# mLSTM scan on one Trainium2 core: states of both directions first, then each chunk once for both

## The chip, the core and the metric

The program runs on one core of one Trainium2 chip. The metric is device time in microseconds (us), from the launch to the end of the program; smaller is better. Five engines work side by side, each with its own queue in its own order: TensorE (PE; its weight loads are listed apart as PEld), VectorE (DVE), ScalarE (ACT), GpSimd (POOL) and SyncE (SP), which issues the transfers. Semaphores tie the queues together.

## The reference, cut to what matters

The program is a two-layer block model (an mLSTM layer and a retention layer, each with a mixture of experts), followed by a block of attention and feed-forward. The change touches the mLSTM scan alone: 8 heads, key width 64, value width 128, 256 context and 512 latent positions, forward and backward. The queries, keys and values of the two directions are the same; only the gates differ. The reference takes chunks of 64 positions.

```python
def mlstm_scan(q, k, v, ig, lf, state):
...
    def step(carry, inp):
        C, n, m = carry
        qc, kc, vc, ic, fc = inp
        b = jnp.cumsum(fc, axis=-1)
        dmat = jnp.where(tril, b[..., :, None] - b[..., None, :] + ic[..., None, :], -jnp.inf)
        inter = b + m[..., None]
        m_row = jnp.maximum(inter, dmat.max(-1))
        s = jnp.einsum('bhid,bhjd->bhij', qc, kc) * jnp.exp(dmat - m_row[..., None])
        w_inter = jnp.exp(inter - m_row)
        num = jnp.einsum('bhij,bhjv->bhiv', s, vc) + w_inter[..., None] * jnp.einsum('bhid,bhdv->bhiv', qc, C)
        den = s.sum(-1) + w_inter * jnp.einsum('bhid,bhd->bhi', qc, n)
        h = num / jnp.maximum(jnp.abs(den), jnp.exp(-m_row))[..., None]
...
        C_new = wc[..., None, None] * C + jnp.einsum('bhj,bhjd,bhjv->bhdv', wk, kc, vc)
...
    oc_f, s = scan_f(ctx_f, state0)
    ol_f, _ = scan_f(lat_f, s)
    oc_b, s = scan_b(flip(ctx_b), state0)
    ol_b, _ = scan_b(flip(lat_b), s)
    return oc_f + jnp.flip(oc_b, 2), ol_f + jnp.flip(ol_b, 2)
...
        y = y * lax.rsqrt(jnp.mean(y * y, axis=-1, keepdims=True) + EPS)
        y = y.reshape(b_, t_, h_ * d_) * norm_g.astype(f32) * jax.nn.sigmoid(o.astype(f32))
```

## The kernel before, in words

The kernel runs the scan in six chunks of 128 positions (two of context, four of latent). `mlstm` (L369) projects the inputs: `qk` holds queries (column blocks 0 to 3) and keys (4 to 7) transposed, two heads of 64 rows to a block of 128 partitions; `v` holds the values with a 129th column for the denominator; `sigo` holds the output gate. `mlstm_gates` (L486) makes from the gates, for both directions, the small tables that the scan reads: `rowt`, `wint` (as three bf16 parts), `colt`, `wk`, `em`, `wcc`, the causal mask, the selectors `sel3`, and `hm`, two columns that are one on the upper or the lower 64 partitions.

`mlstm_scan` (L599) goes through six steps `s`; in each it takes one chunk forward and one backward (orders 0 to 5, and 1, 0, 5, 4, 3, 2), each in two halves `g` of four heads: 24 units. A unit makes the exponents' rows (`rb`, L621 and L623, bf16), keys masked to one head's 64 rows (`kz`, L627, ACT), the products `sc` of keys and queries (L631, over all 128 partitions, the other head's rows being zero), W = Exp (L634, ACT, one per head), P = `sc` times W (L636, DVE); from step 1 on `qb` (L641) and the weighted, masked queries `qw` (L645, DVE); up to step 4 the new state: transposed keys `kt` (L650), `kw` (L652, DVE), `kv` (L657), and C (L662, DVE). Then per pair of heads `o` = P·v (L669) plus `qw`·C (L671), the denominator (Abs on ACT, L673; maximum and reciprocal on DVE), and `o` over the denominator into `y`, or into `yt` and added by POOL or DVE when the other direction came first (L678, L680). After a chunk's second visit `mlstm_finish` (L692) squares `y` (ACT), sums (DVE), takes Sqrt (`rstd`, L95; ACT loads another table for it, and Exp's again after it) and multiplies gate and norm in (POOL L700, L701, DVE L703).

`fill(2)` (L138) advances `ada_mix` (L204) between units: eight weight loads of 1 MB through a ring of four slots, their matmuls L216, and a last step. `ada_close` runs what is left of it after the scan. Buffers: `sc` 2, `rb` 1, `mm` 2 (shared by `qb`, `kt` and `kv`), `o` 2, one for `ada_mix`: eight PSUM banks. A planner at build time sets the order on each engine from the program's order, the buffers and estimated durations, so units are interleaved in the queues. What comes next is `moe0` (L904) with the output projection; its memory is what the scan's inputs leave free.

Of the kernel before, what the change touches and what calls it, by code (L numbers as in the profile page):

```python
# [6 lines left out]
F32 = mybir.dt.float32  # L7
# [5 lines left out]
ALU = mybir.AluOpType  # L13
# [34 lines left out]
class Net:  # L48
# [83 lines left out]

    def ada_close(self):
        self.fill(1000)
        self.aps.close()
        self.ap.close()
# [232 lines left out]
    def mlstm(self):  # L369
# [113 lines left out]
        self.ada_close()  # L483
        return yp, y

    def mlstm_gates(self, G, gp):  # L486
# [16 lines left out]
        hm = gp.tile([128, 2], F32, name="hm")  # L503
        nc.vector.memset(hm, 0.0)
        nc.vector.memset(hm[0:64, 0:1], 1.0)
        nc.vector.memset(hm[64:128, 1:2], 1.0)
# [90 lines left out]
        self.gates = sel3, hm, mask, dirs  # L597

    def mlstm_scan(self, qk, v, gates, y, sigo):  # L599


        nc, I = self.nc, self.I
        NC = 6
        sel3, hm, mask, dirs = gates
        wpool = self.pool("sc_w", 2)
        ng = wpool.tile([128, D], F32, name="ng", bufs=1)
        nc.sync.dma_start(ng, I["mlstm_head_norm_g"][0].partition_broadcast(128))
        pso = self.pool("sc_pso", 2, space=PSUM)
        ps = self.pool("sc_ps", 1, space=PSUM)
        tok = lambda c: slice(128 * c, 128 * c + 128) if c < 2 else slice(128 * c + 2, 128 * c + 130)  # L610
        state = {}
        seen = set()
        for s in range(NC):
            for d in range(2):
                order, rowt, wint, colt, wk, em, wcc = dirs[d]
                c = order[s]
                for g in range(2):
                    pairs = (2 * g, 2 * g + 1)
                    sc = ps.tile([128, 2, 2, 128], F32, name="sc", bufs=2)
                    rb = ps.tile([128, 4, 128], F32, name="rb")  # L620
                    nc.tensor.matmul(rb, self.identb, mask[:, d], start=True, stop=False)  # L621
                    for a in range(4):
                        nc.tensor.matmul(rb[:, a, :], sel3[:, 4 * g + a, :], rowt[:, 128 * c:128 * c + 128],  # L623
                                         start=False, stop=a == 3)
                    kz = wpool.tile([128, 2, 2, 128], F32, name="kz")
                    for e in range(2):
                        nc.scalar.activation(kz[:, :, e, :], qk[:, 4 + 2 * g:6 + 2 * g, tok(c)], AF.Copy,  # L627
                                             scale=hm[:, e:e + 1])
                    for a, p in enumerate(pairs):
                        for e in range(2):  # L630
                            nc.tensor.matmul(sc[:, a, e, :], kz[:, a, e, :], qk[:, p, tok(c)], start=True, stop=True)  # L631
                    W = wpool.tile([128, 4, 128], F32, name="W")
                    for a in range(4):
                        nc.scalar.activation(W[:, a, :], rb[:, a, :], AF.Exp, bias=colt[:, c, 4 * g + a:4 * g + a + 1])  # L634
                    P = wpool.tile([128, 2, 2, 128], F32, name="P")
                    nc.vector.tensor_tensor(P.rearrange("p a e i -> p (a e) i"), sc.rearrange("p a e i -> p (a e) i"), W,  # L636
                                            ALU.mult)
                    if s:
                        qb = ps.tile([128, 2, 128], F32, name="mm", bufs=2)
                        for a, p in enumerate(pairs):  # L640
                            nc.tensor.matmul(qb[:, a, :], sel3[:, 8 + p, :], wint[:, 128 * c:128 * c + 128],  # L641
                                             start=True, stop=True)
                        qw = wpool.tile([128, 2, 2, 128], F32, name="qw")
                        for e in range(2):
                            nc.vector.scalar_tensor_tensor(qw[:, :, e, :], qk[:, 2 * g:2 * g + 2, tok(c)], hm[:, e:e + 1],  # L645
                                                           qb, ALU.mult, ALU.mult)
                    if s < NC - 1:
                        kt = ps.tile([128, 2, 128], F32, name="mm", bufs=2)
                        for a, p in enumerate(pairs):
                            nc.tensor.transpose(kt[:, a, :], qk[:, 4 + p, tok(c)], self.ident)  # L650
                        kw = wpool.tile([128, 4, 64], F32, name="kw")
                        nc.vector.tensor_tensor(kw, kt.rearrange("p a (b e) -> p (a b) e", b=2),  # L652
                                                wk[:, c, 4 * g:4 * g + 4][:, :, None].to_broadcast([128, 4, 64]),
                                                ALU.mult)
                        kv = ps.tile([128, 2, 129], F32, name="mm", bufs=2)
                        for a in range(4):
                            nc.tensor.matmul(kv[64 * (a % 2):64 * (a % 2) + 64, a // 2, :], kw[:, a, :],  # L657
                                             v[:, c, 4 * g + a, :], start=True, stop=True)
                        C = wpool.tile([128, 2, 129], F32, name=f"C{d}{g}")
                        if s:  # L660
                            for a, p in enumerate(pairs):
                                nc.vector.scalar_tensor_tensor(C[:, a, :], state[d, g][:, a, :], wcc[:, p, c:c + 1],  # L662
                                                               kv[:, a, :], ALU.mult, ALU.add)
                        else:
                            nc.vector.tensor_copy(C, kv)
                    for a, p in enumerate(pairs):
                        o = pso.tile([128, 2, 129], F32, name="o")
                        for e in range(2):
                            nc.tensor.matmul(o[:, e, :], P[:, a, e, :], v[:, c, 2 * p + e, :], start=True, stop=not s)  # L669
                            if s:  # L670
                                nc.tensor.matmul(o[:, e, :], qw[:, a, e, :], state[d, g][:, a, :], start=False, stop=True)  # L671
                        den = wpool.tile([128, 2], F32, name="den")
                        nc.scalar.activation(den, o[:, :, 128], AF.Abs)  # L673
                        nc.vector.tensor_tensor(den, den, em[:, c, 2 * p:2 * p + 2], ALU.max)
                        nc.vector.reciprocal(den, den)
                        yy = y[:, c, 2 * p:2 * p + 2, :]
                        dst = wpool.tile([128, 2, 128], F32, name="yt") if (c, g) in seen else yy
                        nc.vector.tensor_tensor(dst, o[:, :, 0:128], den[:, :, None].to_broadcast([128, 2, 128]), ALU.mult)  # L678
                        if (c, g) in seen:
                            (nc.vector if s == NC - 1 else nc.gpsimd).tensor_add(yy, yy, dst)  # L680
                    if s < NC - 1:
                        state[d, g] = C
                    seen.add((c, g))
                    self.fill(2)
# [1612 lines left out]
```

## Time and profile before

| | |
|---|---|
| Median of three runs | 2613.2 us (2613.12 to 2621.31) |
| The profiled execution's own time | 2618.2 us |
| Its span, first to last instruction | 2616.4 us |
| Busy in the span | PE 2496.6 us (95%), DVE 1089.2 (42%), ACT 690.6 (26%), POOL 556.5 (21%) |
| Mean granted TensorE clock | 0.978 of full speed |
| HBM | 567.70 MB read, 223 GB/s over the span |

Busy is the time in which an engine has at least one instruction in work. Matmuls are pipelined and overlap, so a busy PE says less than the distance between two starts. An engine's share over the whole span is a mean of stages with different limits; the scan is one short stage and has to be read by itself.

### The profile page before, as it was taken

To read this page: it belongs to the slowest core of one execution; us is meant where nothing else is said; L and a number is where in the kernel's file an instruction comes from. 1 tells how busy PE (TensorE), PEld (TensorE's weight loads), DVE (VectorE), ACT (ScalarE), POOL (GpSimd) and SP (SyncE) were. 2 spreads that over 40 slices of the span, in tenths; PEclk is the share of its full clock that TensorE was granted. 3 is DMA by queue.
4 is the path that set the end of the run, shared out by engine and by line. 5 is a ranking of instruction groups with operands and counts; after the bars stand their busy time and mean duration, and the time that the engine had idled before them with its cause. 6 is when DMAs were issued, how large, how long until landed. Compare 5 with 4: busy or idle time off the path is not lost. (4 is left out here: it accounts for less than half of the span.)

```text
span 2616.4 us, 36613 instructions
## 1 busy us (share of the span) xinstructions
PE 2496.6 (95%) x15126; PEld 1612.8 (62%) x15126; DVE 1089.2 (42%) x2121; ACT 690.6 (26%) x1335; POOL 556.5 (21%) x339
## 2 busy tenths in 40 slices
PE   7999898989999999999999999999998999999999
PEld 6777586834443333378787755444445766788887
DVE  6578687341111111143766332222235558433310
ACT  4322365421111111044224310000013446322211
POOL 2213325311111110124556200000001212122233
PEclk9989999989999999999999999999998999999999
DMA  7216604388999999442564489999982231133331
GB/s 255 80 51 211 231 26 151 126 327 334 393 393 396 395 402 408 154 135 71 180 222 174 190 360 420 420 419 420 420 339 93 81 98 33 57 97 97 121 105 57
DMA packets 145274, 584.80 MB, mean 224 GB/s; under 512 B 17671, under 2 KB 47535, under 8 KB 93908
## 3 DMA queue, kind: packets, MB, share of 16 engines
q1 hardware_dynamic: 138684, 569.87, 57.0%
q0 software_dynamic: 6416, 12.59, 2.2%
q8 instruction: 119, 1.95, 0.3%
q14 instruction: 47, 0.39, 0.0%
q10 hardware_dynamic: 8, 0.01, 0.0%
HBM read 567.70 MB, written 14.71 MB: 223 GB/s over the span
## 5 line engine op out<-in xcount | busy, mean ns | idle before, releaser
L276 POOL TENSOR_TENSOR wlo<-w,whi 128x1024 fp32r<-128x1024 f32 x103 | 270.6, 2628 | 614.6 <-ACT whi L275 613.6
L872 PE MATMUL pl<-w,xT 128*64 128x512 f32 x1240 | 289.0, 599 | 2.7 <-ACT hl L1355 2.7
L275 ACT ACTIVATE whi<-w 128x1024 fp32r<-128x1024 f32 x148 | 154.4, 1049 | 456.7 <-PE acc L296 191.1
L294 PE MATMUL acc<-whi,hhi 128*128 128x512 f32 (+2 forms) x672 | 267.0, 398 | 1.1 <-ACT pre L445 1.1
L295 PE MATMUL acc<-wlo,hhi 128*128 128x512 f32 (+2 forms) x672 | 262.9, 391 | 1.2 <-POOL wlo L276 1.2
L296 PE MATMUL acc<-whi,hlo 128*128 128x512 f32 (+2 forms) x672 | 261.5, 390 | 0.0
L296 PE MATMUL acc<-hhi,wlo 128*128 128x512 f32 (+2 forms) x528 | 198.8, 377 | 3.2 <-POOL wlo L276 3.2
L294 PE MATMUL acc<-hhi,whi 128*128 128x512 f32 (+2 forms) x528 | 199.1, 378 | 2.9 <-DVE hlo L289 1.5
L295 PE MATMUL acc<-hlo,whi 128*128 128x512 f32 (+2 forms) x528 | 199.0, 377 | 0.6 <-POOL hlo L406 0.5
L872 PEld LDWEIGHTS pl<-w,xT 128*64 128x64 f32 x1240 | 90.4, 137 | 159.1 <-issue 148.8
L276 DVE TENSOR_TENSOR wlo<-w,whi 128x1024 fp32r<-128x1024 f32 (+2 forms) x45 | 59.3, 1317 | 256.3 <-ACT whi L275 256.1
L872 PE MATMUL pl<-wb,xT 128*64 128x512 f32 x640 | 151.4, 597 | 0.0
L294 PEld LDWEIGHTS acc<-whi,hhi 128*128 128x128 f32 x672 | 128.3, 191 | 30.0 <-issue 6.1
L295 PEld LDWEIGHTS acc<-wlo,hhi 128*128 128x128 f32 x672 | 128.8, 192 | 27.0 <-POOL wlo L276 2.8
L296 PEld LDWEIGHTS acc<-whi,hlo 128*128 128x128 f32 x672 | 128.5, 191 | 25.7 <-issue 2.4
L164 DVE SCALAR_TENSOR_TENSOR ada_v<-w,csil,ada_v 128x1024 f32<-128x1024 f32 x84 | 133.1, 1619 | 8.1 <-DMA w<-in_ada_w_dram 6.8
L1813 POOL TENSOR_TENSOR X<-X,s_gf 128x1024 f32<-128x1024 f32 x2 | 4.7, 2370 | 515.0 <-ACT s_sq L1812 506.2
L294 PEld LDWEIGHTS acc<-hhi,whi 128*128 128x128 f32 (+1 forms) x528 | 98.4, 187 | 22.4 <-DVE hlo L289 1.7
L296 PEld LDWEIGHTS acc<-hhi,wlo 128*128 128x128 f32 (+1 forms) x528 | 98.2, 186 | 22.5 <-POOL wlo L276 3.4
L295 PEld LDWEIGHTS acc<-hlo,whi 128*128 128x128 f32 (+1 forms) x528 | 98.3, 186 | 19.8 <-POOL hlo L406 0.7
L872 PEld LDWEIGHTS pl<-wb,xT 128*64 128x64 f32 x640 | 47.7, 137 | 81.4 <-issue 75.3
L1041 ACT ACTIVATE xT<-ro_tp,cols,ffnA 128x32 f32<-128x32 f32 x128 | 43.7, 376 | 199.7 <-DVE xT L1038 195.6
(599 smaller groups left out, 4252.6 us busy)
## 6 DMA issues: line engine op xcount, KB each, us to landing
w<-in_moe_w_gate_dram SPq DMA_DIRECT2D x91, 1024.0 KB, 13.9
w<-in_moe_w_down_dram SPq DMA_DIRECT2D x84, 1024.0 KB, 15.1
w<-in_moe_w_up_dram SPq DMA_DIRECT2D x68, 1024.0 KB, 19.8
wb<-in_moe_w_up_dram SPq DMA_DIRECT2D x53, 1024.0 KB, 13.2
w<-in_ada_w_dram SPq DMA_DIRECT2D x40, 1024.0 KB, 6.0
wb<-in_moe_w_down_dram SPq DMA_DIRECT2D x38, 1024.0 KB, 21.9
wb<-in_moe_w_gate_dram SPq DMA_DIRECT2D x30, 1024.0 KB, 19.9
w<-in_ret_w_in_dram SPq DMA_DIRECT2D x16, 1024.0 KB, 5.7
```

Of the source, the lines that this page charges most:

```text
L164: nc.vector.scalar_tensor_tensor(acc[r], w[:, kk], x, acc[r], ALU.mult, ALU.add)
L275: nc.scalar.activation(hi, raw[:, k:k + n, :], AF.Copy)
L276: (nc.vector if fast and (k // n) % 2 == 0 else nc.gpsimd).tensor_sub(lo, raw[:, k:k + n, :], hi.bitcast(F32))
L294: nc.tensor.matmul(out, lh[0], rh[0], start=start, stop=False)
L295: nc.tensor.matmul(out, lh[0], rh[1], start=False, stop=False)
L296: nc.tensor.matmul(out, lh[1], rh[0], start=False, stop=stop)
L872: self.nc.tensor.matmul(out[64 * b:64 * b + 64, :], lat(kk), w[:, kk - k0, 512 * c:512 * c + 512], start=kk == 0, stop=kk == KD - 1)
L1041: nc.scalar.activation(xT[:, kk, a:b], tp[:, k, a:b], AF.Identity, scale=A[:, kk, 1:2], bias=B[:, kk, 1:2])
L1813: (nc.gpsimd if t % 3 else nc.vector).tensor_mul(x, x, gf)
```

## The change: what it does

The scan falls into two stages. The first (the state stage) goes through steps 0 to 4 of both directions and makes only the states: four transposes, one `kw` over all eight heads, `kv` into four banks, and C, one tile per direction and step, all kept. `fill(1)` stands between the ten units, and what is left of `ada_mix` runs at its end, where its PSUM bank is closed. The gains are multiplied into `sigo` there.

The second (the chunk stage) takes chunks 0 to 5, each once. The key-query products are computed once per chunk for both directions, head by head on the 64 partitions where that head lies, into two banks (`sc0`, `sc1`), without `kz`. Four units follow (half `g`, direction `d`): `rb`, W, P in two parts, once per direction `qb` and an unmasked `qw`, then `o` in two banks, one for the upper and one for the lower heads, with `qw`·C on 64 partitions. Forward results are copied to `y` by ACT with the scale 1/den; backward ones are multiplied and added by DVE in one instruction. Each chunk is finished right after. PSUM: `sc` 2 banks, `rb` (shared with `qb`) 2, `o` 4.

```diff
-    def ada_close(self):
-        self.fill(1000)
-        self.aps.close()
-        self.ap.close()
...
         qp.close()
-        self.ada_close()
+        self.ap.close()
...
-        hm = gp.tile([128, 2], F32, name="hm")
...
+        sp = self.pool("sc_C")
+        wpool = self.pool("sc_wA", 2)
         ng = wpool.tile([128, D], F32, name="ng", bufs=1)
         nc.sync.dma_start(ng, I["mlstm_head_norm_g"][0].partition_broadcast(128))
...
+        row = (slice(0, 64), slice(64, 128))
+        before = {}
+        ps = self.pool("sc_psA", 1, space=PSUM)
+        for s in range(NC - 1):
             for d in range(2):
                 order, rowt, wint, colt, wk, em, wcc = dirs[d]
                 c = order[s]
+                kt = ps.tile([128, 4, 128], F32, name="kt", bufs=2)
+                for p in range(4):
+                    nc.tensor.transpose(kt[:, p, :], qk[:, 4 + p, tok(c)], self.ident)
+                kw = wpool.tile([128, 8, 64], F32, name="kw")
+                nc.vector.tensor_tensor(kw, kt.rearrange("p a (b e) -> p (a b) e", b=2),
+                                        wk[:, c, :, None].to_broadcast([128, 8, 64]), ALU.mult)
+                C = sp.tile([128, 4, 129], F32, name=f"C{d}{s}")
                 for g in range(2):
+                    kv = ps.tile([128, 2, 129], F32, name="kv", bufs=4)
+                    for a in range(4):
+                        h = 4 * g + a
+                        nc.tensor.matmul(kv[row[a % 2], a // 2, :], kw[:, h, :], v[:, c, h, :], start=True, stop=True)
+                    if s:
+                        for a in range(2):
+                            p = 2 * g + a
+                            nc.vector.scalar_tensor_tensor(C[:, p, :], before[d, c][:, p, :], wcc[:, p, c:c + 1],
+                                                           kv[:, a, :], ALU.mult, ALU.add)
+                    else:
+                        nc.scalar.copy(C[:, 2 * g:2 * g + 2, :], kv)
+                before[d, order[s + 1]] = C
+                self.fill(1)
+            nc.gpsimd.tensor_mul(sigo[:, s, :], sigo[:, s, :], ng)
+        nc.gpsimd.tensor_mul(sigo[:, NC - 1, :], sigo[:, NC - 1, :], ng)
+        ps.close()
+        wpool.close()
+        wpool = self.pool("sc_w", 2)
+        self.fill(1000)
+        self.aps.close()
+        pso = self.pool("sc_pso", 4, space=PSUM)
+        ps = self.pool("sc_ps", 1, space=PSUM)
+        for c in range(NC):
+            sc = [ps.tile([128, 4, 128], F32, name=f"sc{e}") for e in range(2)]
+            for p in range(4):
+                for e in range(2):
+                    nc.tensor.matmul(sc[e][:, p, :], qk[row[e], 4 + p, tok(c)], qk[row[e], p, tok(c)], start=True, stop=True)
+            qw = {}
+            for g in range(2):
+                for d in range(2):
+                    order, rowt, wint, colt, wk, em, wcc = dirs[d]
+                    C = before.get((d, c))
+                    heads = [(e, a, 4 * g + 2 * a + e) for e in range(2) for a in range(2)]
+                    rb = ps.tile([128, 4, 128], F32, name="rb", bufs=2)
                     nc.tensor.matmul(rb, self.identb, mask[:, d], start=True, stop=False)
+                    for e, a, h in heads:
+                        nc.tensor.matmul(rb[:, 2 * e + a, :], sel3[:, h, :], rowt[:, 128 * c:128 * c + 128],
+                                         start=False, stop=(e, a) == (1, 1))
+                    W = wpool.tile([128, 2, 2, 128], F32, name="W")
+                    for e, a, h in heads:
+                        nc.scalar.activation(W[:, e, a, :], rb[:, 2 * e + a, :], AF.Exp, bias=colt[:, c, h:h + 1])
+                    P = wpool.tile([128, 2, 2, 128], F32, name="P")
                     for e in range(2):
+                        nc.vector.tensor_tensor(P[:, e], sc[e][:, 2 * g:2 * g + 2, :], W[:, e], ALU.mult)
+                    if g == 0 and C is not None:
+                        qb = ps.tile([128, 4, 128], F32, name="rb", bufs=2)
+                        for p in range(4):
+                            nc.tensor.matmul(qb[:, p, :], sel3[:, 8 + p, :], wint[:, 128 * c:128 * c + 128],
+                                             start=True, stop=True)
+                        qw[d] = wpool.tile([128, 4, 128], F32, name="qw", bufs=3)
+                        nc.vector.tensor_tensor(qw[d], qk[:, 0:4, tok(c)], qb, ALU.mult)
+                    o = [pso.tile([128, 2, 129], F32, name="o") for _ in range(2)]
+                    for a in range(2):
+                        p = 2 * g + a
                         for e in range(2):
+                            nc.tensor.matmul(o[e][:, a, :], P[:, e, a, :], v[:, c, 2 * p + e, :], start=True, stop=C is None)
+                        for e in range(2 if C is not None else 0):
+                            nc.tensor.matmul(o[e][:, a, :], qw[d][row[e], p, :], C[row[e], p, :], start=False, stop=True)
+                    den = wpool.tile([128, 2, 2], F32, name="den")
+                    for e in range(2):
+                        nc.scalar.activation(den[:, e], o[e][:, :, 128], AF.Abs)
+                    nc.vector.tensor_tensor(den, den, em[:, c, 4 * g:4 * g + 4].rearrange("p (a e) -> p e a", e=2), ALU.max)
+                    nc.vector.reciprocal(den, den)
+                    for e, a, h in heads:
+                        yy, oo, r = y[:, c, h, :], o[e][:, a, 0:128], den[:, e, a:a + 1]
+                        if d == 0:
+                            nc.scalar.activation(yy, oo, AF.Copy, scale=r)
                         else:
+                            nc.vector.scalar_tensor_tensor(yy, oo, r, yy, ALU.mult, ALU.add)
+            self.mlstm_finish(c, y, sigo, wpool)
...
-        nc.gpsimd.tensor_mul(sigo[:, t, :], sigo[:, t, :], ng)
         nc.gpsimd.tensor_mul(sigo[:, t, :], sigo[:, t, :], yf)
```

## Rows read from the trace of the kernel before

**Rows 1.** Table by stretches: stretch, length, busy per engine (instructions), clock, DMA, GB/s.

```profile
292.60:325.30 32.70, 28.43 (x202) 15.21 (x202) 17.15 (x36) 13.78 (x43) 13.93 (x6) 0.95 0.60 214
...
340.00:357.00 17.00, 14.65 (x133) 12.62 (x132) 16.05 (x42) 13.88 (x34) 6.14 (x5) 1.00 0.01 2
...
376.00:395.00 19.00, 19.00 (x179) 16.82 (x178) 14.89 (x49) 10.26 (x34) 4.39 (x5) 1.00 0.00 1
...
395.00:414.00 19.00, 15.69 (x132) 13.91 (x131) 17.80 (x53) 14.59 (x36) 7.69 (x7) 0.96 0.00 1
```

**Rows 2.** PE in order of time, 376 to 379 us: start, length, engine, line, operation, count.

```profile
376.22 0.66 PE L657 MATMUL mm<-v,kw 128*64 128x129 f32 x8
376.81 0.49 PE L671 MATMUL o<-C,qw 128*128 128x129 f32 x2
377.14 0.39 PE L669 MATMUL o<-v,P 128*128 128x129 f32 x2
377.36 0.39 PE L671 MATMUL o<-C,qw 128*128 128x129 f32 x2
377.58 0.28 PE L641 MATMUL mm<-wint,sel 96*128 96x128 bf16 x2
377.70 0.38 PE L621 MATMUL rb<-mask,identb 128*128 128x512 bf16 x1
377.92 0.38 PE L650 MATMUL mm<-cs,qk 128*128 128x128 f32 x2
378.13 0.39 PE L623 MATMUL rb<-rowt,sel 96*128 96x128 bf16 x4
378.36 0.66 PE L631 MATMUL sc<-qk,kz 128*128 128x128 f32 x4
```

**Rows 3.** PE in order of time: last `ada_mix` run, last `o` row.

```profile
322.08 1.92 PE L216 MATMUL ada_acc<-w,ada_sc 128*32 128x512 f32 x14
...
420.45 0.39 PE L671 MATMUL o<-C,qw 128*128 128x129 f32 x2
```

**Rows 4.** PE in order of time, later attention stage (`da_s`), 2200 to 2212 us.

```profile
2200.07 0.70 PE L2118 MATMUL da_s<-s_kT,s_qT 64*128 64x256 f32 x2
...
2201.81 0.70 PE L2118 MATMUL da_s<-s_kT,s_qT 64*128 64x256 f32 x4
...
2211.01 0.49 PE L2118 MATMUL da_s<-s_kT,s_qT 64*128 64x128 f32 x4
2211.43 0.44 PE L2148 MATMUL da_t<-cs,da_x 128*128 128x128 f32 x2
```

**Rows 5.** Groups by line, ACT, 292.6 to 434 us: busy, mean ns, idle before.

```profile
L634 ACT ACTIVATE W<-rb,colt 128x128 f32<-128x128 f32 x96 | 27.7, 366 | 9.9 <-PE rb L623 9.8
...
L673 ACT ACTIVATE den<-o 128x2 f32<-128x2 f32 x48 | 8.2, 172 | 36.5 <-PE o L671 25.1 <-PE o L669 11.1
...
L99 ACT ACT_TABLE_LOAD x5 | 6.4, 1283 | 0.1
...
L697 ACT ACTIVATE mf_sq<-y 128x1024 f32<-128x1024 f32 x6 | 6.3, 1057 | 2.6 <-DVE y L680 2.0 <-POOL y L680 0.5
...
L99 ACT ACTIVATE rs_t<-mf_ss,epsc 128x8 f32<-128x8 f32 x6 | 1.8, 301 | 1.9 <-DVE mf_ss L698 1.9
```

**Rows 6.** Groups by line, DVE, 292.6 to 434 us.

```profile
L636 DVE TENSOR_TENSOR P<-sc,W 128x512 f32<-128x512 f32 x24 | 16.4, 682 | 3.7 <-ACT W L634 3.7
...
L678 DVE TENSOR_TENSOR y<-o,den 128x256 f32<-128x256 f32 x24 | 10.0, 420 | 1.0
...
L662 DVE SCALAR_TENSOR_TENSOR C<-C,wcc,mm 128x129 f32<-128x129 f32 x32 | 9.7, 344 | 1.1 <-PE mm L657 0.8
...
L698 DVE TENSOR_REDUCE mf_ss<-mf_sq 128x8 f32<-128x1024 f32 x6 | 7.3, 1214 | 2.1 <-ACT mf_sq L697 2.0
```

**Rows 7.** PE in order of time, the row behind a long idle stretch.

```profile
412.46 0.73 PE L669 MATMUL o<-v,P 128*128 128x129 f32 x2 [2.07 <-DVE yt L678]
```

**Rows 8.** Table by stretches, the 4 us around that row.

```profile
412.00:416.00 4.00, 3.54 (x16) 3.47 (x16) 2.98 (x7) 1.12 (x2) 2.35 (x1) 0.57 0.00 0
```

More of the change, by code (lines that the diff above doesn't have):

```diff
@@ L502, in mlstm_gates @@
             nc.vector.tensor_copy(sel3[32 * a:32 * a + 8, 8:12, :], psel)
-        hm = gp.tile([128, 2], F32, name="hm")
-        nc.vector.memset(hm, 0.0)
-        nc.vector.memset(hm[0:64, 0:1], 1.0)
-        nc.vector.memset(hm[64:128, 1:2], 1.0)
         def parts(x, name):
@@ L596, in mlstm_gates @@
         g0.close()
-        self.gates = sel3, hm, mask, dirs
+        self.gates = sel3, mask, dirs
     def mlstm_scan(self, qk, v, gates, y, sigo):
@@ L603, in mlstm_scan @@
         NC = 6
-        sel3, hm, mask, dirs = gates
-        wpool = self.pool("sc_w", 2)
+        sel3, mask, dirs = gates
+        sp = self.pool("sc_C")
+        wpool = self.pool("sc_wA", 2)
         ng = wpool.tile([128, D], F32, name="ng", bufs=1)
         nc.sync.dma_start(ng, I["mlstm_head_norm_g"][0].partition_broadcast(128))
-        pso = self.pool("sc_pso", 2, space=PSUM)
-        ps = self.pool("sc_ps", 1, space=PSUM)
         tok = lambda c: slice(128 * c, 128 * c + 128) if c < 2 else slice(128 * c + 2, 128 * c + 130)
-        state = {}
-        seen = set()
-        for s in range(NC):
+        row = (slice(0, 64), slice(64, 128))
+        before = {}
+        ps = self.pool("sc_psA", 1, space=PSUM)
+        for s in range(NC - 1):
             for d in range(2):
@@ L616, in mlstm_scan @@
                 c = order[s]
-                for g in range(2):
-                    pairs = (2 * g, 2 * g + 1)
-                    sc = ps.tile([128, 2, 2, 128], F32, name="sc", bufs=2)
-                    rb = ps.tile([128, 4, 128], F32, name="rb")
-                    nc.tensor.matmul(rb, self.identb, mask[:, d], start=True, stop=False)
[L622 to L625, printed above, removed]
-                    for e in range(2):
-                        nc.scalar.activation(kz[:, :, e, :], qk[:, 4 + 2 * g:6 + 2 * g, tok(c)], AF.Copy,
-                                             scale=hm[:, e:e + 1])
-                    for a, p in enumerate(pairs):
-                        for e in range(2):
[L631 to L663, printed above, removed]
-                        else:
[L665 to L684, printed above, removed]
@@ L685, in mlstm_scan @@
-                if (c, "half") in seen:
-                    self.mlstm_finish(c, y, sigo, ng, wpool)
-                seen.add((c, "half"))
+                kt = ps.tile([128, 4, 128], F32, name="kt", bufs=2)
[4 more added lines that the diff above has]
+                                        wk[:, c, :, None].to_broadcast([128, 8, 64]), ALU.mult)
@@ L690, in mlstm_scan, with mlstm_finish @@
         wpool.close()
-    def mlstm_finish(self, t, y, sigo, ng, pool):
+        sp.close()
+    def mlstm_finish(self, t, y, sigo, pool):
         nc = self.nc
```

## The prediction, made before the changed kernel was built or run

> **What bounds the kernel now.** I read the page for the whole, then the table by stretches for the stage the diff rewrites, then the groups of instructions by line, then single rows in order of time. The first stretch begins with the scan, at 292.6 us, and the last `o` row runs from 420.45 for 0.39 [rows 1, 3]: 128.2 us, 4.9% of the span. Nothing else in the program changes, and what follows starts when the scan's memory comes free, so a microsecond of scan is a microsecond of the total.
>
> Inside the scan PE is the bound. From 376 to 395 us it is busy 19.00 of 19.00 us, with DVE at 14.89 and ACT at 10.26 [rows 1]. It is not full everywhere: 28.43 of 32.70 us while step 0 runs, and 14.65 of 17.00 and 15.69 of 19.00 us in two stretches that each hold two chunk finishes (their sums, and Sqrt between two table loads) [rows 1]. The reader is to see that a finish costs PE (2.35+3.31)/4 = 1.4 us, and that DVE and ACT have slack only while PE is the slowest.
>
> Matmul durations overlap, so I cost PE by the distance from one start to the next. A 128-column f32 product is two instructions, 0.22 us apart from the next product (377.14 to 377.36); the pair of `qb` matmuls takes 0.12, the mask matmul 0.22, two transposes 0.21, four row matmuls 0.23, eight `kv` instructions 0.59 [rows 2]. Behind `kv`, whose outputs are 64 columns wide, the next product takes 0.33 instead of 0.22 [rows 2]: changing the shape of the array costs 0.1 us. Fourteen `ada_mix` instructions take 1.92, 0.137 each [rows 3].
>
> With the counts of the loops (24 units of direction, step and half of the heads): mask 24 x 0.22 = 5.3; row matmuls 24 x 0.23 = 5.5; `sc` 192 x 0.112 = 21.5; `qb` 20 x 0.12 = 2.4; transposes 20 x 0.21 = 4.2; `kv` 20 x (0.59 + 0.2 for two changes) = 15.8; `P·v` 192 x 0.112 = 21.5; `qw·C` 160 x 0.112 = 17.9 (an f32 product is two instructions, so 24 x 4 products are 192); `ada_mix` 64 x 0.137 + 0.4 + 8 x 0.2 = 10.8. That is 104.9 us of PE in 128.2; 23.3 us are waits.
>
> **The change part by part.**
>
> *Shared 64-row products.* `sc` is computed once per chunk, not once per direction: 48 products instead of 96, and each on 64 rows, upper and lower half of the array in turn. Whether two halves run at once, the `da_s` rows of the later attention tell: two instructions on one half (64x256) take 0.70 us, four on both halves also 0.70 [rows 4]. So pairs overlap. Four 64x128 instructions occupy 0.42 us to the next start (2211.01 to 2211.43) [rows 4]; at full overlap two times 0.11 would do, and the other 0.2 is the change of shape before and after. New `sc`: 16 instructions in one run per chunk, 0.88 + 0.2 = 1.08, six times: 6.5 instead of 21.5 us, 15.0 saved.
>
> *`qw·C` on 64 rows.* 40 pairs, each between two full-height `P·v` products, so each pays the change twice: 40 x 0.42 = 16.8 instead of 17.9 us, 1.1 saved. The overlap is eaten by the changes. The Trainium skill (TensorEngine Tiling (Array Packing), section Key Properties) says that a change of tiling mode drains the engine; this speaks against the change, and the trace agrees, with 0.1 us. With the 128-cycle drain that TensorE: Matmul & The Clock Gate (the Trainium skill, Phases on the wall clock) gives, an estimate of 0.053 us each, the 92 new changes would cost 4.9 instead of 9.2 us and the total would be 4 us lower; I keep the row.
>
> *Other matmuls* keep number and size. PE's sum becomes 104.9 - 16.1 = 88.8 us: 30.8 in the state stage (transposes, `kv`, `ada_mix`) and 58.0 in the chunk stage, 9.7 a chunk.
>
> *ACT.* Removed: the 48 `kz` copies. Kept: 96 W, 27.7 us; 48 Abs, 8.2; Squares 6.3; six Sqrt, 1.8 [rows 5]. Table loads: 12, since each chunk now has a finish of its own, instead of five before Sqrt and five back to Exp, at 1.283 [rows 5]: 15.4. Added: 48 copies of `o` times 1/den for the forward direction, which DVE did. No row shows that form; bounds are 0.17 (Abs, two columns) and 0.37 (one W by itself) [rows 5]; I take W's 27.7/96 = 0.29, the same 128 columns from PSUM in groups of four: 13.9. Sum 73.3 us, and all of it in the chunk stage: 12.2 a chunk. So ACT, not PE, is the floor there.
>
> *DVE.* `qw` loses its masking: 10 multiplies of 512 columns at 0.68 (P's shape) = 6.8. The C updates are unchanged, 32 of 0.344. `yt` and its add become one 128-column operation per head, backward only: 48 x 0.344 (the C update's shape) = 16.5. P in halves: 48 x 0.42 (the 256 columns of L678) = 20.2. Finish: sum and closing multiply, 1,024 columns each and counted alike, 6 x 2 x 1.21 = 14.5 (all durations: [rows 6]). That is 58.0 us, 9.7 a chunk; the 48 short operations on denominators, half as many as now, would have to take 0.3 us each to lift DVE to ACT's 12.2. State stage: 10 `kw` of 512 columns x 0.68 + 32 x 0.344 = 17.8, beside 30.8 of PE.
>
> *Moves at nothing.* The gain multiplies on POOL (L700) start when `ng` lands, as now; the chunk stage's memory waits for them, and by step 0 of before they are over long before the state stage ends. `ada_mix`'s eight weight loads stay on SP in the same order; `fill(1)` ten times instead of `fill(2)` 24 times spreads the same nine steps over ten units of about 3 us; if a load were late, PE would wait for it there, up to the 4.3 us that step 0 shows [rows 1]. POOL's adds of `y` go; POOL is no bound.
>
> **The sum.** State stage 30.8 + 1.5 (first transpose, multiply, `kv`). Handing over: the chunk stage uses the same PSUM banks, so its first `o` matmul waits for row matmuls 0.45, W 1.15 and P 0.8 less what `sc` covers: 2.6. Chunks: bounds are 12.2 us (ACT's floor) and 15.9. The upper one is two units in flight (`W`, `P`, `rb` are two deep, `o` four banks): a unit's chain is row matmuls 0.45, W 1.15, P 0.84, `o` 2 x (0.45 + 0.42) = 1.74, Abs of two banks 0.25, maximum and reciprocal (counted like Abs) 0.34, four copies or updates 1.3, hand-overs 0.4: 6.5, so 3.25 a unit, 13.0 for four, and 2.9 for Sqrt and its two table loads in ACT's queue. I take 13.0, near the floor, because the old scan, with buffers no deeper and a chain as long, kept its slowest engine busy 100% away from finishes [rows 1]; the 0.8 is what the finish cost PE, less the part that the table loads already put in ACT's floor. Total 30.8 + 1.5 + 2.6 + 78.0 = 112.9 against 128.2: 15.3 us less. The profiled execution took 2618.2 us (span 2616.4), so it would be 2602.9; the three runs' median is 2613.2, hence **2598 us**.
>
> **Rivals.**
> - *The engines overlap better*: ACT's busy times overlap by a tenth, 11 us a chunk: 100.9, 2586 us. For it: four W's fit in 1.15; against it: three engines within 2.5 us of each other.
> - *Two units in flight are the bound*: 15 to 15.9 a chunk, 124.9 to 130.3: 2610 to 2615 us, no change. For it: ACT now stands twice in every unit's chain. Against it: 100% of PE above.
> - *The halves don't run at once*, because the order of PE's queue splits pairs (a single half cost as much as two [rows 4]): `sc` +5.4, `qw·C` 40 x 0.23 = +9.2, PE 12.1 a chunk, level with ACT; 14.2 a chunk, 2605 us.
> - *PE's clock falls.* PE idled for 2.07 us until 412.46, and from 412 to 416 the mean granted clock was 0.57 [rows 7, 8]: 86% of 4 us at the lower level, 1.2 GHz, so 1.7 us were lost. Once per chunk, at the table loads, that is 10.2 us: 2608 us. The Trainium skill (TensorE: Matmul & The Clock Gate, HAM oscillation) says that gaps between bursts bring half clock back each time. Against it: 340 to 357 us held two finishes at clock 1.00 [rows 1].
> - *Slower: the finish blocks ACT's queue.* If Square, Sqrt and the table loads of chunk c stand ahead of W of chunk c+1, no W is made from c's last `o` matmul on: Abs, maximum, reciprocal (counted alike) 0.5, four updates 1.1, Square 1.06, sum 1.21, two tables and Sqrt 2.87, hand-overs 0.6: 7.3, plus W and P 1.8, less two buffered units of `o`, 3.5: 5.6 instead of 1.4 a chunk, 17.2: 138.1, 2623 us. It is slower than before from 15.6 a chunk on. Against it: in 395 to 414 us ACT is 14.59 busy with two finishes [rows 1], so other work passed between.
>
> **Chances.** Forecast (12.2 to 14.2 a chunk, 2593 to 2605) 0.55; better overlap 0.10; two in flight 0.15; halves apart 0.05; clock 0.05; slower 0.10. A measurement of this kernel tells 0.3%, 7.8 us, from no change. Faster: 0.55 + 0.10 + 0.03 of the halves apart, whose 2605 is at that line: 0.68. Same: 0.02 of these, 0.13 of two in flight, 0.04 of the clock: 0.19. Slower: 0.10 and the 0.03 left of these two: 0.13. The range goes from better overlap with a little to spare to just past two in flight: 2582 to 2616.
>
> **What would show it.** Right: a state stage of 32 to 35 us with PE busy over 85%; then six like periods of about 13 us, ACT busy over 85% and PE about 75%; `sc` in runs of 16 instructions near 1.1 us; no `kz`; 12 table loads. Wrong: PE starts of `sc` 0.11 apart (halves apart); clock below 1.00 in the chunk stage; ACT idle while a finish is under way (slower); or a state stage longer than 40 us, waiting for weights.

## The result: slower, 2663.6 against 2615.5 us

The changed kernel's median is 2663.6 us (2661.3 to 2665.5, four runs), the kernel before 2615.5 us (2613.1 to 2621.3, four runs): a ratio of 1.0186, 95% interval 1.0172 to 1.0200. The forecast was 2598 us, its range 2582 to 2616.

The profiled execution has a span of 2661.7 us, 45.3 longer than before. The first two lines below are its page's span and busy times; the third is the granted clock in 40 slices of 67 us.

```profile
span 2661.7 us, 36283 instructions
...
PE 2536.5 (95%) x15030; PEld 1627.3 (61%) x15030; DVE 1061.6 (40%) x2042; ACT 686.1 (26%) x1341; POOL 544.8 (20%) x323
...
PEclk9999975899999999999999999999999999999999
```

PE's share is 95% as before, and the page gives only one hint: slices 6 to 8 (333 to 532 us) have clock digits 7, 5 and 8. The table by stretches (stretch, length, busy of PE, PEld, DVE, ACT and POOL with instructions, clock, DMA, GB/s) shows where they lie. It is cut at the starts of the key-query products, so a row is the state stage, then each of the six chunks, then the output projection.

```profile
293.90:323.10 29.20, 28.11 (x269) 15.08 (x268) 15.69 (x45) 2.55 (x7) 13.99 (x6) 1.00 0.85 297
323.10:338.40 15.30, 12.66 (x99) 10.07 (x101) 6.15 (x20) 9.56 (x35) 0.00 (x0) 0.89 0.15 46
338.40:356.50 18.10, 13.45 (x85) 10.19 (x81) 8.76 (x27) 10.06 (x33) 2.37 (x1) 0.78 0.00 0
356.50:379.30 22.80, 20.73 (x110) 15.47 (x110) 10.44 (x29) 11.47 (x37) 2.36 (x1) 0.72 0.00 1
379.30:406.90 27.60, 26.18 (x112) 18.87 (x111) 10.09 (x29) 11.68 (x37) 2.36 (x1) 0.56 0.00 1
406.90:434.80 27.90, 26.48 (x112) 19.11 (x111) 10.09 (x29) 11.62 (x36) 2.36 (x1) 0.56 0.00 1
434.80:462.50 27.70, 26.36 (x109) 18.61 (x107) 10.09 (x29) 11.62 (x36) 2.36 (x1) 0.56 0.00 1
462.50:497.00 34.50, 30.46 (x132) 23.56 (x132) 20.63 (x32) 15.70 (x31) 21.96 (x15) 0.80 0.74 283
```

The state stage took 29.2 us at full clock, 3.1 less than forecast. The six chunks took 139.4 us in place of 78.0, the later ones 27.7 each, with PE over 94% busy, ACT and DVE under 45%, and the clock at 0.56. The scan is 168.6 us instead of 128.2 [rows 1, 3]: 40 of the 45 us.

PE's queue in order of time, at full clock (compare [rows 2]) and at half clock (columns: start, length, engine, line, operation, count):

```profile
362.52 0.49 PE L673 MATMUL o<-v,P 128*128 128x129 f32 x2
362.94 0.49 PE L675 MATMUL o<-C,qw 64*128 64x129 f32 x2
363.35 0.49 PE L673 MATMUL o<-v,P 128*128 128x129 f32 x2
363.77 0.49 PE L675 MATMUL o<-C,qw 64*128 64x129 f32 x2
...
394.70 0.80 PE L673 MATMUL o<-v,P 128*128 128x129 f32 x2
395.43 0.80 PE L675 MATMUL o<-C,qw 64*128 64x129 f32 x2
396.16 0.80 PE L673 MATMUL o<-v,P 128*128 128x129 f32 x2
```

A count of 2 is one f32 product. One full-height product and one 64-row product alternate: of the 80 `qw·C` products 52 stand alone in the queue and 28 in 14 pairs. Each starts 0.42 us behind the last, where full-height products alone had 0.22 [rows 2], and 0.73 at half clock.

What is around the falls of the clock, in the same kernel: the idle row of PE behind the first finish, and single stretches of 2 us.

```profile
349.30 0.59 PE L652 MATMUL rb<-mask,identb 128*128 128x512 bf16 x1 [3.93 <-ACT W L658]
```

```profile
346.00:348.00 2.00, 0.00 (x0) 0.00 (x0) 1.56 (x4) 1.99 (x5) 0.00 (x0) 1.00 0.00 0
348.00:350.00 2.00, 0.70 (x3) 0.42 (x3) 1.82 (x7) 2.00 (x9) 0.00 (x0) 0.65 0.01 4
350.00:352.00 2.00, 2.00 (x7) 1.32 (x7) 0.64 (x2) 0.28 (x2) 0.00 (x0) 0.50 0.00 0
356.00:358.00 2.00, 2.00 (x17) 1.78 (x18) 1.01 (x5) 0.80 (x5) 0.00 (x0) 0.50 0.00 0
358.00:360.00 2.00, 1.24 (x13) 0.89 (x12) 1.18 (x4) 0.95 (x4) 1.40 (x1) 0.79 0.00 0
```

PE waits 3.93 us for W, which stands behind the finish in ACT's queue; the clock falls to half (0.50, that is 1.2 GHz) and stays there although PE is busy without a break, until the next chunk's run of key-query products (from 356.50) has gone through. From chunk 3 on half clock takes nearly the whole chunk. There PE has no long gap any more: in the last three chunks its waits are short ones, for `qw` (2.3 us in all) and P (1.8; P stands behind the finish's sum in DVE's queue). The clock of chunk 3 falls behind two of them and stays down while PE is busy without a break:

```profile
383.39 0.38 PE L652 MATMUL rb<-mask,identb 128*128 128x512 bf16 x1 [0.78 <-DVE qw L668]
384.85 0.49 PE L673 MATMUL o<-v,P 128*128 128x129 f32 x2 [0.64 <-DVE P L661]
```

```profile
384.00:386.00 2.00, 1.36 (x10) 0.93 (x7) 2.00 (x5) 1.94 (x4) 0.00 (x0) 1.00 0.00 0
386.00:388.00 2.00, 2.00 (x10) 1.44 (x8) 1.48 (x3) 1.92 (x3) 0.00 (x0) 0.54 0.04 8
390.00:405.00 15.00, 15.00 (x52) 10.44 (x50) 3.14 (x12) 4.77 (x21) 0.00 (x0) 0.50 0.00 0
```

### The profile page after: what moved, and what is told of

The parts are those of the page before. It is cut to its first block, busy times and chain, and to the rows that moved or that the text cites. A ratio compares the mean times of both kernels' runs of the same rounds, so it can differ in the third digit from the quotient of the medians.

```text
span 2661.7 us, 36283 instructions
## 1 busy us (share of the span) xinstructions
PE 2536.5 (95%) x15030; PEld 1627.3 (61%) x15030; DVE 1061.6 (40%) x2042; ACT 686.1 (26%) x1341; POOL 544.8 (20%) x323
## 5 line engine op out<-in xcount | busy, mean ns | idle before, releaser
L291 PEld LDWEIGHTS acc<-whi,hlo 128*128 128x128 f32 x672 | 128.2, 191 | 26.0 <-issue 2.4
## 6 DMA issues: line engine op xcount, KB each, us to landing
w<-in_moe_w_gate_dram SPq DMA_DIRECT2D x91, 1024.0 KB, 13.9
w<-in_moe_w_down_dram SPq DMA_DIRECT2D x84, 1024.0 KB, 15.1
wb<-in_moe_w_up_dram SPq DMA_DIRECT2D x53, 1024.0 KB, 13.5
wb<-in_moe_w_gate_dram SPq DMA_DIRECT2D x30, 1024.0 KB, 20.2
```

Of the source, the lines that this page charges most:

```text
L291: nc.tensor.matmul(out, lh[1], rh[0], start=False, stop=stop)
```

## The experiments

Theory 1: the 64-row products that stand alone between full-height ones cost PE time, and their thin stream takes its clock. Theory 2: the finish blocks ACT, PE idles, and that lets the clock fall. Theory 3: ACT's chain and two units in flight set the chunk's length. The table holds what was measured: the median, the ratio to the kernel before (95% interval), and, from each run's profile, the length of the chunk stage (first key-query product to last `o` product) and its mean granted clock.

| Run | PE's order or height | us | ratio | chunk stage, us | clock |
|---|---|---|---|---|---|
| the change | 64-row `qw·C`, most of them alone | 2663.6 | 1.0186 (1.0172 to 1.0200) | 139.4 | 0.65 |
| e1_all_full | all full height | 2609.4 | 0.998 (0.997 to 0.999) | 92.0 | 0.93 |
| e2_state_full | `qw·C` full height | 2615.4 | 1.001 (1.000 to 1.002) | 91.1 | 0.94 |
| e3_scores_full | `sc` full height | 2659.9 | 1.016 (1.013 to 1.019) | 145.2 | 0.65 |
| e4_paired | four and four | 2618.2 | 1.002 (1.000 to 1.003) | 98.8 | 0.86 |
| e9_pairs | two and two | 2633.4 | 1.007 (1.005 to 1.009) | 113.8 | 0.75 |
| e8_single | one and one | 2652.6 | 1.014 (1.012 to 1.016) | 135.8 | 0.75 |
| e5_finish_last | as the change | 2635.4 | 1.007 (1.005 to 1.010) | 114.5 | 0.79 |
| e6_filler | as the change, plus dense work | 2636.6 | 1.007 (1.005 to 1.009) | 129.2 | 0.87 |
| e7_one_in_flight | `qw·C` full height | 2629.8 | 1.006 (1.004 to 1.008) | 102.9 | 0.90 |
| b0_masked | `qw·C` full height | 2618.9 | 1.002 (1.001 to 1.003) | 102.3 | 0.88 |
| b1_masked_full | `qw·C` full height | 2618.1 | 1.002 (1.001 to 1.003) | 89.8 | 0.93 |
| b6_short_chain | `qw·C` full height | 2616.5 | 1.000 (0.999 to 1.001) | 90.6 | 0.92 |

In these profiled executions the scan begins between 289.7 and 296.2 us, with nothing ahead of it changed, so a few us between two kernels need not be the scan's.

### Which product

```diff
# e1: both lines; e3: the first alone; e2: the second alone
-  nc.tensor.matmul(sc[e][:, p, :], qk[row[e], 4 + p, tok(c)], qk[row[e], p, tok(c)], start=True, stop=True)
+  nc.tensor.matmul(sc[e][:, p, :], qk[:, 4 + p, tok(c)], qk[:, p, tok(c)], start=True, stop=True)
-  nc.tensor.matmul(o[e][:, a, :], qw[d][row[e], p, :], C[row[e], p, :], start=False, stop=True)
+  nc.tensor.matmul(o[e][:, a, :], qw[d][:, p, :], C[:, p, :], start=False, stop=True)
```

> The changed kernel with all 128 rows in both 64-row products, the key-query one (L644) and `qw*C` (L675): same number of instructions, same queue order, same finish, but no product of the chunk stage has another array shape (the output then holds the other head's part too; only its time is read). Theory 1 (a 64-row product that stands alone between full-height ones costs far more than half of a pair, and the thin stream that results takes TensorE's granted clock down): about 2605 us (2590 to 2620), clock 0.98 or more, chunk periods of 13 to 15 us in place of 22 to 28. Theory 2 (the finish in ACT's queue starves PE and that lets the clock fall): the finish is untouched, so 2645 to 2665 us. Theory 3 (ACT's chain and two units in flight bound the chunk stage): 2640 or more as well.

> Only `qw*C` (L675) with all 128 rows (40 pairs of products; they then hold the other head's part too); the shared key-query products stay 64 rows high. Theory 1: nearly all of the loss sits in the products that are split by the queue, since the 16 key-query products of a chunk stand together and took 1.06 to 1.16 us: about 2600 us (2585 to 2615), clock 0.98 or more. Theories 2 and 3: 2640 us or more.

> The counterpart: only the key-query products (L644) with all 128 rows (they then hold both heads' part), `qw*C` stays at 64 rows. Theory 1: nothing gets better, 2655 to 2680 us (the run of 16 takes some 2 us more a chunk, unless a fuller PE keeps its clock). Theories 2 and 3: 2655 to 2670 us too; the run only tells which of the two products carries the loss.

Full-height `qw·C` alone takes away 48 of the 48 us, full-height `sc` next to none. The finish is the same in all three, so theory 2 by itself falls. The time of e2 is at the edge of what was expected; it is no faster than before, and its chunk is 15.2 us, not 13. In e1 and e2 the clock of the chunk stage is 0.93 and 0.94, under the 0.98 that was expected. That e1 is 6 us faster than e2, with a chunk stage no shorter, is not explained by the runs. e2's profile shows the same idle gap at the first finish, and another sequel (PE's row, then stretches of 4, 4 and 2 us):

```profile
345.78 0.38 PE L652 MATMUL rb<-mask,identb 128*128 128x512 bf16 x1 [3.65 <-ACT W L658]
```

```profile
342.00:346.00 4.00, 0.35 (x5) 0.10 (x2) 3.38 (x12) 3.97 (x15) 0.00 (x0) 1.00 0.01 2
346.00:350.00 4.00, 4.00 (x23) 4.00 (x22) 1.20 (x4) 1.11 (x5) 0.00 (x0) 0.57 0.00 0
350.00:352.00 2.00, 2.00 (x29) 1.76 (x28) 0.52 (x4) 1.27 (x7) 0.00 (x0) 1.00 0.00 0
```

The gap costs half clock here too, but a stream of full-height products has the full clock again by 350 us. In the changed kernel the same gap brought some 10 us at half clock. Nor does every wait of PE bring half clock: e2 holds 1.00 from 350 to 400 us, through waits of up to 2.3 us (its longest wait there: total, times, longest; and the stretch around it).

```profile
PE rb L652 <- ACT den L678: 2.3, 1, 2.3
350.00:365.00 15.00, 10.69 (x100) 9.26 (x99) 10.27 (x31) 11.36 (x36) 2.37 (x1) 1.00 0.00 1
```

### Only the order

The three kernels have the scores in one tile and one P instruction a unit; e9 and e8 differ from e4 only in the order of the same products in PE's queue (the edits are shortened here).

```diff
# e4, in a unit that carries a state
+  for a in range(2):
+      for e in range(2): P*v(e, a)        # start=a == 0
+  for a in range(2):
+      for e in range(2): qw*C(e, a)       # 64 rows, stop=a == 1
# e9: for a: P*v(0, a), P*v(1, a), qw*C(0, a), qw*C(1, a)
# e8: for a: for e: P*v(e, a), qw*C(e, a)
```

> The changed kernel's arithmetic with another order: the scores in one tile of two banks, one P instruction for a unit in place of two, and in PE's queue first the four P*v of a unit, then its four 64-row `qw*C` side by side, so that two changes of the array's shape stand in a unit in place of four. Theory 1: a large part comes back, 2600 to 2635 us, `o` work of a unit 1.5 to 2.2 us in place of 3.4 at full clock. Theories 2 and 3: 2640 us or more.

> The same kernel in the order that the prediction assumed: two P*v, then the pair of `qw*C`, twice in a unit, so four changes of shape in place of two or eight. Theory 1, by the distance that the other traces show between products (0.22 us within one shape, about 0.2 more at a change): 20 units x 2 more changes x 0.2 = 8 us over the paired run at full clock, so 2622 to 2640 us, and between the two others in clock as well. If the order doesn't count: 2612 to 2625 us.

> The kernel of the paired run (scores in one tile, one P instruction a unit) with one thing changed: a 64-row `qw*C` stands alone behind each P*v in PE's queue, eight changes of array shape in a unit that carries a state in place of two. Theory 1: the cost goes by the changes, so this one is as slow as the changed kernel, 2645 to 2670 us, with products 0.42 us apart at full clock. If what counts is that the products are 64 rows high, whatever their order, it is like the paired run, 2612 to 2625 us; if P in two halves or the scores' two tiles made the loss, also 2612 to 2625 us.

2618, 2633 and 2653 us for two, four and eight changes of array shape in a unit: all in the ranges of theory 1. The order of PE's queue alone makes 34 us. It acts in two ways: e4's 98.8 us at a clock of 0.86 and e9's 113.8 at 0.75 are both some 85 us' worth of full clock, so what e9 loses is clock; e8's 135.8 at the same 0.75 are 102, so there it is time at PE. The count of changes doesn't set the time by itself: the changed kernel has fewer than e8 (135 against 163 in the chunk stage), a lower clock (0.65 against 0.75), and is 11 us slower. Why its clock is down for longer than e8's the runs don't show.

The prices come from PE's rows at full clock, e4 and then e9 (a count of 8 is four products, 4 is two):

```profile
367.32 1.13 PE L671 MATMUL o<-v,P 128*128 128x129 f32 x8 [0.22 <-DVE P L660]
368.38 0.71 PE L676 MATMUL o<-C,qw 64*128 64x129 f32 x8
369.03 1.16 PE L671 MATMUL o<-v,P 128*128 128x129 f32 x8
```

```profile
343.48 0.68 PE L671 MATMUL o<-v,P 128*128 128x129 f32 x4 [0.82 <-DVE P L660]
344.09 0.49 PE L675 MATMUL o<-C,qw 64*128 64x129 f32 x4
344.52 0.71 PE L671 MATMUL o<-v,P 128*128 128x129 f32 x4
```

A unit takes 1.71 us (367.32 to 369.03) with two changes and 2 x 1.04 = 2.08 with four: 0.19 a change between these products. Without changes the 1.71 would be 1.33, that is 0.88 for four full-height products and 0.45 for two 64-row pairs: pairs do overlap fully, as the prediction had it. Singles, with eight changes, take 8 x 0.42 = 3.36: four more changes are 0.76, and the other 0.52 is put down to the overlap that single halves lose (two more products at 0.22 would be 0.44).

### The finish, and filling PE

```diff
# e5
-            self.mlstm_finish(c, y, sigo, wpool)
+        for c in range(NC):
+            self.mlstm_finish(c, y, sigo, wpool)
# e6
+  for _ in range(4):
+      nc.tensor.matmul(rb, self.identb, mask[:, d], start=True, stop=True)
   nc.tensor.matmul(rb, self.identb, mask[:, d], start=True, stop=False)
```

> The changed kernel with all six finishes (Square, sums, Sqrt, the closing multiplies) taken out of the chunk loop and done behind it; nothing else moves. PE's queue and ACT's hold no finish, and no table load, among the chunks. Theory 1 (the 64-row products that stand alone between full-height ones cost PE the time and its clock): the chunk stage stays at 20 us or more a chunk with the clock near 0.5 to 0.6 in long stretches; 2650 to 2675 us, since the finishes now lie behind the last product. Theory 2 (the finish blocks ACT's queue, PE idles and its clock falls): the clock stays near 1.00 and the chunk stage takes about 13 us a chunk; 2615 us or less even with the finishes at the end.

> The changed kernel with useless work added on PE: four more full-height bf16 products of 512 columns (the mask product again, overwritten) ahead of each unit's exponents, 24 x 4 x 0.22 = 21 us of PE at full clock. What the traces of the runs so far suggest (theory 1 in a sharper form): an idle gap of PE brings the clock to half, and the stream of single 64-row and full-height products doesn't bring it back, while a dense run does. Then dense filler in each unit gives the clock back and the kernel gets faster by doing more: 2630 to 2648 us, mean clock of the chunk stage 0.80 or more in place of 0.65. If the time were the changes of shape alone and the clock a side effect, the filler adds its own time: 2675 to 2705 us.

e5 misses both ranges: 28 us faster than the change, still 21 us behind the kernel before. So the finish had a part, which theory 1 had left out; with full-height `qw·C` (e2) the finishes stay where they are and nothing is lost against the kernel before. In its sharper form (an idle gap starts half clock, single products keep it there, dense work ends it) it was put to e6, which adds 21 us of work on PE (96 products at 0.22) and is 27 us faster than the change. Neither run isolates its cause, for the planner's order moved as well: 25 pairs of `qw·C` in e5 and 26 in e6, against 14, and 113 changes of shape in the chunk stage against 135, some 4 us at 0.19. In the profiled executions of e6 and the change, 25 us apart, the chunk stage accounts for 10.2; 4.2 lie ahead of the scan and 4.5 between the last `o` and the first expert product. The clock does go from 0.65 to 0.87, and e6's profile shows it return within the chunk.

```profile
362.00:364.00 2.00, 0.01 (x1) 0.01 (x1) 0.42 (x1) 1.92 (x8) 0.00 (x0) 1.00 0.00 0
364.00:366.00 2.00, 2.00 (x8) 1.58 (x8) 1.27 (x3) 1.02 (x4) 0.00 (x0) 0.64 0.00 0
366.00:374.00 8.00, 7.78 (x30) 5.12 (x30) 1.81 (x8) 1.45 (x8) 0.00 (x0) 0.50 0.00 0
374.00:376.00 2.00, 2.00 (x14) 1.12 (x11) 0.42 (x1) 1.25 (x5) 0.00 (x0) 0.80 0.01 4
376.00:380.00 4.00, 4.00 (x40) 3.23 (x38) 1.14 (x5) 0.34 (x4) 0.00 (x0) 1.00 0.02 4
```

### What is left when the clock holds, and a better version

```diff
# e7 (on e2)
-        pso = self.pool("sc_pso", 4, space=PSUM)
+        pso = self.pool("sc_pso", 2, space=PSUM)
# b0 (scores in one tile and one P as in e4, products written as in e9): zeros stay in the other head's rows of qz[d]
+  for e in range(2):
+      nc.vector.tensor_tensor(qz[d][row[e], e], qk[row[e], 0:4, tok(c)], qb[row[e]], ALU.mult)
...
+  nc.tensor.matmul(o[e][:, a, :], qz[d][:, e, p, :], C[:, p, :], start=False, stop=True)
# b1 (on b0): Square, sum and gate in the chunk; one Sqrt and six closing multiplies behind the last chunk
# b6 (on b0): the same in two groups of three chunks, and without Abs on ACT
+  nc.vector.scalar_tensor_tensor(den, last, -1.0, em..., ALU.mult, ALU.max)
+  nc.vector.tensor_tensor(den, den, last, ALU.max)
```

> The run with full-height `qw*C` (which holds its clock and still takes 15.2 us a chunk, with no engine full) with two PSUM banks for `o` in place of four: one unit in flight between its products and its updates. If the chain of a unit (products, Abs, maximum, reciprocal, four updates) and the two units in flight are what sets those 15.2 us, the chunk goes to 18 to 22 us and the time to 2632 to 2660 us. If it is an engine's sum of work or the finish, the depth hardly counts: 2612 to 2622 us.

> The masked full-height version with the finish left in the chunk loop as in the changed kernel (its counterpart with the finish split off ended its last product no earlier and then idled for 12 us). Theory 1: as the run with unmasked full-height `qw*C`, plus at most 1.1 us a chunk on DVE: 2610 to 2622 us, clock 0.97 or more. If the 64-row height is not the cause: 2640 us or more.

> An attempt at a version that beats both: the state stage and the shared 64-row key-query products (a run of 16 a chunk) of the changed kernel; `qw` with zeros in the other head's rows, so that `qw*C` is full height (DVE writes two masked halves, 6.8 us more in all); one P instruction a unit; and of the finish only Square, sums and the gate's multiply stay in the chunk, while one Sqrt for all six chunks and the closing multiplies stand at the end (two table loads in place of twelve). Theory 1: PE needs about 10.4 us a chunk, ACT 9.5, DVE 10; the clock holds, chunks of 11 to 13 us, 2585 to 2602 us. If two units in flight are the bound: 13 us and more a chunk, 2600 to 2612 us.

> A second attempt at a version that beats both: masked full-height `qw*C`, one P instruction, the denominators wholly on DVE (two short instructions on a two-bank tile in place of two Abs on ACT and one on DVE, so one hop between engines less in every unit's chain), and the Sqrt of three chunks at a time (four table loads in place of twelve). If the chain of two units in flight is the floor: about 0.5 us less per unit and pair in flight, 1 us a chunk, and 1 us a chunk from the table loads: 13 us a chunk, 2598 to 2610 us. If the floor is elsewhere (DVE, at about 11.5 us a chunk here, or what follows the scan): 2610 to 2620 us.

One unit in flight costs 14 us over e2, between its two ranges and just under the one that theory 3 gave, and part of it is clock (0.90 against 0.94). Two in flight thus bear on the 15.2 us a chunk, but the runs don't settle what sets them: with two table loads in place of twelve (b1) the chunk is 15.0, with a hop less and four table loads (b6) 15.1, against 17.1 in b0, and PE, the busiest engine in both, is at about 79%. b0's time is in its range, but its clock (0.88) is not the 0.97 that was expected.

Neither version beats the kernel before. b6 falls in the range of its rival, a floor elsewhere. b1 misses both its ranges: its last product ends 9 us earlier than the scan of before, then PE stands still for the closing multiplies (second row).

```profile
322.00:411.80 89.80, 70.63 (x604) 62.48 (x608) 54.02 (x140) 52.27 (x198) 12.99 (x8) 0.93 0.02 7
411.80:424.00 12.20, 0.04 (x1) 0.00 (x0) 11.96 (x16) 7.41 (x13) 9.12 (x5) 0.64 0.43 163
```

## Why the prediction was wrong, step by step

**State stage: right in kind, 3.1 us shorter.** 29.2 us against 30.8 + 1.5, PE 96% busy. The shared key-query products are right as well: at full clock a run of 16 instructions lasts 1.06 to 1.16 us, against 1.08.

```profile
323.13 1.16 PE L644 MATMUL sc<-qk 64*128 64x128 f32 x16 [1.12 <-DVE C L624]
...
338.38 1.06 PE L644 MATMUL sc<-qk 64*128 64x128 f32 x16
```

**ACT and DVE: right in size.** The first three rows answer to [rows 5], the last two to [rows 6] (line, operation, count, busy, mean ns, idle before). The unknown copies took 13.7 us against 13.9, the backward updates 13.5 against 16.5, P in halves 19.4 against 20.2. That they decide nothing is the point: ACT waited for `o` instead.

```profile
L658 ACT ACTIVATE W<-rb,colt 128x128 f32<-128x128 f32 x96 | 28.9, 380 | 7.7 <-PE rb L654 7.5
L684 ACT ACTIVATE y<-o,den 128x128 f32<-128x128 f32 x48 | 13.7, 371 | 1.0 <-DVE den L680 1.0
L678 ACT ACTIVATE den<-o 128x2 f32<-128x2 f32 x48 | 6.9, 171 | 56.0 <-PE o L675 47.2 <-issue 8.0 <-PE o L673 0.7
```

```profile
L661 DVE TENSOR_TENSOR P<-sc,W 128x256 f32<-128x256 f32 x48 | 19.4, 418 | 24.5 <-ACT W L658 22.9 <-PE o L673 0.7
L686 DVE SCALAR_TENSOR_TENSOR y<-o,den,y 128x128 f32<-128x128 f32 x48 | 13.5, 343 | 1.1 <-ACT y L684 0.4
```

**The step that failed: "`qw·C` on 64 rows. 40 pairs, each between two full-height `P·v` products, so each pays the change twice: 40 x 0.42 = 16.8".** The term assumed 40 pairs; the queue has 14, and 52 products alone. Adjacent in the program is not adjacent in the queue that the planner makes. ([rows 2] could not show it: there `P·v` and `qw·C` alternate because the old program is written so.) And the 0.1 us a change, read behind `kv`, was half of the 0.19 measured here; the pairs' overlap was right. A pair or a single between full-height products takes about 0.60 (1.04 - 2 x 0.22 in e9; 2 x 0.42 - 0.22 alone), so the 66 take some 40 us where the term had 16.8: some 23 more, by this estimate.

The second half of the failure is that the sum charged the whole chunk stage at full clock: 78.0 us with 58.0 of PE in them, and a chance of 0.05 for a fall of the clock. By the six rows PE was busy for 125.9 of the 139.4 us. At the mean clock of 0.65 the stage is 91 us' worth of full clock; 13 of them are the 13.5 us in which PE was idle, nearly all at full clock. That leaves 78 us' worth of work, 20 more than the sum had, and 48 us that its busy time lost to the clock. Idle time was 13.5 us where the sum left 20.0. So of the 61.4 us that the stage took beyond the forecast, the clock is 48, by far the most. Pairs as the term had them would not have saved the forecast: e9 has that order, and takes 19.0 us a chunk at a clock of 0.75, 2633.4 us in all.

**The rivals were right in kind and too small.** "The halves don't run at once, because the order of PE's queue splits pairs" was priced at 9.2 us for the lost overlap; it left out that each single product would then pay for two changes of its own. "PE's clock falls" was priced at 1.7 us a gap, from a gap that full-height products followed [rows 7, 8], and set against a stretch of before that held full clock through two finishes [rows 1]. Both conditions changed with the stream: half clock lasted 10 us and more behind a gap, and from chunk 3 on it came behind waits of under 0.8 us.

**The forecast's 13.0 us a chunk was too short even so.** With the clock nearly held (e2) it is 15.2, in the rival's 15 to 15.9 for two units in flight, and the time is 2615 us, no change. Of the 8.6 us by which e2's last product comes earlier (412.0 against 420.6 us), 3.6 were left at the first expert product (533.2 against 536.8 us).

On the pages cited: the Trainium skill (TensorEngine Tiling (Array Packing), section Key Properties) says that a change of tiling mode drains the engine; the runs agree that a change costs time, 0.19 us here. The estimate of 0.053 us from TensorE: Matmul & The Clock Gate (the Trainium skill, Phases on the wall clock) was 3.5 times too low. The same page's HAM oscillation lets gaps bring half clock each time; the trace agrees for the gap of 3.93 us, and the runs add that what PE does around a gap counts as well: in the change waits of 0.78 and 0.64 us stood before a fall, in e2 one of 2.3 us brought none.

## What to carry to other kernels

Before pricing a product that uses part of the array, read its neighbours in PE's queue from the trace, product by product, and count the changes of shape in the order the planner makes, not in the order of the program. Group such products, or make them full height: four side by side (2618.2 us) and masked, full-height ones (2618.9) were alike here, and faster than pairs (2633.4). Price a stall of PE together with the stream behind it: after a like gap the change had half clock for 10 us, e2 for under 4.

## What the runs showed that had not been expected

- PE listed as busy without a break, as in 350 to 358 us and 390 to 405 us of the change, can stay at half clock: the profile's busy share says nothing of whether the clock will rise.
- More work on PE went with a faster kernel: 21 us of filler, 27 us less (2663.6 to 2636.6), of which the chunk stage shows 10.
- The same products in three orders: 2618, 2633 and 2653 us.
- Moving the finish out of the chunk loop went with 28 us less where `qw·C` has 64 rows (e5). With full-height ones, and the Sqrt made once (b0 to b1), the chunk stage fell by 12.5 us and the whole by 0.8, since PE then waited 12 us behind it.
